# One pair of experts instead of two kept for the down products by columns at the end

## The chip, the core and the metric

The kernel runs on one core of a Trainium2 chip, in one launch. The metric is device time in microseconds (us). Its engines are TensorE (PE in the profile, with PEld for its weight loads), VectorE (DVE), ScalarE (ACT), GpSimd (POOL) and SyncE (SP), which issues the DMAs of the weights.

## The reference, cut to what matters

One encoder layer on 256 tokens of 1024 channels, all in float32: a mixer block, then a mixture of 32 experts, the residual and a last RMSNorm. The change touches the experts and the norm:

```python
for e in range(N_EXPERTS):                     # 32
    act = silu(t @ w1[e]) * (t @ w3[e])        # 1024 -> 512
    out = out + combine[:, e:e+1] * (act @ w2[e])   # 512 -> 1024
x = x + out
return rmsnorm(x, norm_final_g)
```

A token goes to two experts. The weights w1, w3 and w2 of one expert are 2 MiB each, 192 MiB in all.

## The kernel before

After the mixer and the routing the kernel works through 16 pairs of experts. At most 64 tokens are gathered for an expert (a general path, `general()`, L922, handles more behind a test at run time, and is jumped over here); the two experts of a pair share the 128 columns of every product.

A pair has these steps. `hidden` (L857) computes w1, then w3, 16 matmuls of 512 columns each in the program (the profile shows two passes for each float32 matmul, so 32). ACT applies silu, DVE multiplies (L884). `spread` (L834) transposes the pair's one-hot tokens. `turn` (L887) transposes the activations, and `down` (L901) multiplies them with w2, 16 matmuls of 512 columns. `two` (L896) splits each result in a rounded part (ACT, L897) and the rest (DVE, L898). `combine` (L915) scatters both parts to the 256 tokens with 8 matmuls into the four accumulators `accm`; the program puts it in the middle of the next pair's `hidden`. Every second pair also gathers the tokens of the next four experts (L790).

The weights come through a ring of 22 slots of 1 MiB, in the order of the list `stream` (L56 to L94), in DMAs from SP's queue (L124). A DMA waits until its slot is free and until an earlier DMA on its semaphore has landed; eight semaphores are used in turn. `fill` (L113) issues as many as there are free slots, and is called wherever a step frees some.

The last two pairs, 14 and 15, are treated apart. Their w2 is left out of `seq` (L75) and comes at the very end, in pieces of 256 and 128 columns, pair 14 and pair 15 in turns (L88 to L94). So the program computes w1 and w3 of pair 14, the first matrix of pair 15 with `turn_a` in the middle (L1010), jumps over the general path, adds the accumulators of pairs 0 to 13 to the residual (L1021), computes w3 of pair 15, and then runs the down products of both pairs by columns (`down_col` L1030, `combine_a` L1052, `combine_b` L1058). Behind a column group follow the residual (L1063), its squares (L1068) and, for the second half of the tokens, the product with the last norm's gain (L1071). That gain was spread over all partitions before, by `gains_bcast` (L998, L1001). At last come the sum of squares (L1096), the root, and five scaled pieces with their DMAs (L1106).

The program's order is the order written; no scheduler moves it. The lines that set it at the end are

```python
    a = hidden(NP - 2)
    gwa, gwb = [spread(gts[NP // 2 - 1], i) for i in range(2)]
    gains_bcast(0)
    gains_bcast(1)
    hidden(NP - 1, ("w1",), {("w1", 0): turn_a})
    general()
    ...
    a = hidden(NP - 1, ("w3",))
```

Of the kernel before, what the change touches and what calls it, by code (L numbers as in the profile page):

```python
# [9 lines left out]
FT = mybir.dt.float32  # L10
# [9 lines left out]
P = 128  # L20
# [20 lines left out]
def encoder_kernel(ctx, tc, x, norm_mix_g, w_in, conv_a_w, conv_b_w, conv_b_bias, ln_b_g, ln_b_b,  # L41
# [30 lines left out]
    w2_v = w2[0].rearrange("e (p k) d -> e p k d", k=KF)  # L72
    NP = E_ALL // 2
    W = {"w1": (w1_v, 4), "w3": (w3_v, 4), "w2": (w2_v, 2)}
    seq = [(pr, nm) for pr in range(NP) for nm in ("w1", "w3", "w2") if pr < NP - 2 or nm != "w2"]  # L75
    for q in range(4):
        for e in range(2):
            stream.append((("w1", e, q), w1_v[e][:, 2 * q:2 * q + 2, :], ("w1", q), e * 1024))
# [6 lines left out]
    for q in range(2):  # L85
        for e in (E_ALL - 2, E_ALL - 1):
            stream.append((("w3", e, 1 + q), w3_v[e][:, 4 + 2 * q:6 + 2 * q, :], ("w3", e), q * 1024))
    LAST2 = [(NP - 2, [(0, 256), (256, 256), (512, 256), (768, 256)]),  # L88
             (NP - 1, [(0, 256), (256, 256), (512, 256), (768, 128), (896, 128)])]
    COLS = LAST2[1][1]  # L90
    for i, c in [(0, 0), (1, 0), (0, 1), (1, 1), (0, 2), (0, 3), (1, 2), (1, 3), (1, 4)]:
        pr, (c0, n) = LAST2[i][0], LAST2[i][1][c]
        for e in (2 * pr, 2 * pr + 1):
            stream.append((("w2", e, c), w2_v[e][:, :, c0:c0 + n], ("w2", e, c0 // 512), c0 % 512 * KF))  # L94
    tiles, owner = {}, {}
    free = [(0, n) for n in range(RING)]
    order, shared = [1000], {}
# [2 lines left out]
    def slot(key, dt=FT, name="wt"):  # L100
        free.sort()
        owner[key] = free.pop(0)[1]
        return ring.tile([P, 2048], dt, name=name, tag=f"w{owner[key]}")

    def done(*keys, rank=None):
        for key in keys:
            order[0] += 1
            free.append((rank or order[0], owner.pop(key)))
# [805 lines left out]

    def combine(pr, gw, ys):  # L915
        for h in range(2):
            for nh in range(2):
                for n, y in enumerate(ys[nh]):
                    PE.matmul(accm[h][nh], gw[:, h], y, start=(pr == 0 and n == 0), stop=(pr == NP - 3 and n == 1))  # L919


    def general():  # L922
# [48 lines left out]
        done("gen", "tT")  # L971

    prev = None
    for pr in range(NP - 2):
        q, i = divmod(pr, 2)
        if i:
            gts[q + 1] = onehot(q + 1)
        keep[0] = int(pr == NP - 3)

        def mid():  # L980
            if prev:
                combine(*prev)
            else:
                fs[0] = factors(0, gt0)
        a = hidden(pr, meanwhile={("w1", 1): mid})
        gw = spread(gts[q], i)
        at = turn(a)
        if i:
            for n in range(4):
                gather(gts[q + 1], n)  # L990
            fs[q + 1] = factors(q + 1, gts[q + 1])
        prev = (pr, gw, down(pr, at))
    combine(*prev)
    done("x2h", "x2l")
    xl = slot("xl")
    gfb = xl[:, D:]

    def gains_bcast(nh):  # L998
        p = ps.tile([P, 512], FT, name="gfp", tag="mm")
        for k in range(4):  # L1000
            PE.matmul(p[:, k * P:(k + 1) * P], ident[0:KD, 4 * nh + k:4 * nh + k + 1].to_broadcast([KD, P]),  # L1001
                      gf8, start=True, stop=True)
        S.copy(gfb[:, nh * 512:(nh + 1) * 512], p)

    a = hidden(NP - 2)
    gwa, gwb = [spread(gts[NP // 2 - 1], i) for i in range(2)]
    gains_bcast(0)
    gains_bcast(1)

    def turn_a():  # L1010
        ats.append(turn(a, xl[:, 0:KF * P].rearrange("p (k t) -> p k t", k=KF)))

    ats = []

    hidden(NP - 1, ("w1",), {("w1", 0): turn_a})
    general()
    S.activation(warm, epst, AF.Sqrt)
    for h in range(2):
# [1 line left out]
            sl = slice(nh * 512, (nh + 1) * 512)  # L1020
            V.tensor_tensor(x1[:, h, sl], accm[h][nh], x1[:, h, sl], op=OP.add)  # L1021
    a = hidden(NP - 1, ("w3",))
    atl = turn(a, xl[:, KF * P:2 * KF * P].rearrange("p (k t) -> p k t", k=KF))
    s6 = cst.tile([P, 2, len(COLS)], FT, name="s6")
    xo = slot("xo").rearrange("p (h d) -> p h d", h=2)

    ysl = slot("ysl").rearrange("p (i n) -> p i n", n=256)
    ysr = slot("ysr", FR, "ysr").rearrange("p (i j n) -> p i j n", j=2, n=256)

    def down_col(i, c, at):  # L1030
        pr, cols = LAST2[i]
        n = cols[c][1]
        p = ps.tile([P, n], FT, name="yp", tag="mm")
        for k in range(KF):
            for e in range(2):
                PE.matmul(p[e * CAP:(e + 1) * CAP], at[:, k, e * CAP:(e + 1) * CAP],  # L1036
                          tiles["w2", 2 * pr + e, c][:, k], start=(k == 0), stop=(k == KF - 1))
        if c < 3:
            return two(p, ysr[:, (2 * c + i) % 4, 0], ysr[:, (2 * c + i) % 4, 1])
        ysb = ysl[:, 2 * (c % 4) + i, 0:n]  # L1040
        S.copy(ysb, p)
        return ysb

    def scatter(i, h, c, ysb, start, stop):
        g = (gwa, gwb)[i][:, h]
        parts = [(g, y) for y in ysb] if c < 3 else [(g.bitcast(FT), ysb)]
        for n, (g, y) in enumerate(parts):
            PE.matmul(pls[c, h], g, y, start=start and n == 0, stop=stop and n == len(parts) - 1)  # L1048

    pls = {}  # L1050

    def combine_a(c, ysb):  # L1052
        for h in range(2):
            pool, tag = (pacc, f"acc{h}{c % 2}") if c < 4 else (ps, "h")
            pls[c, h] = pool.tile([P, COLS[c][1]], FT, name="last", tag=tag)
            scatter(0, h, c, ysb, True, False)

    def combine_b(c, ysb):  # L1058
        c0, n = COLS[c]
        sl = slice(c0, c0 + n)  # L1060
        for h in range(2):
            scatter(1, h, c, ysb, False, True)
            V.tensor_tensor(x1[:, h, sl], pls[c, h], x1[:, h, sl], op=OP.add)  # L1063
            if h and c == len(COLS) - 1:
                V.scalar_tensor_tensor(ysl[:, 2, 0:n], x1[:, h, sl], 1.0, x1[:, h, sl], op0=OP.mult, op1=OP.mult,
                                       accum_out=s6[:, h, c:c + 1])
            else:
                S.activation(xo[:, 0, sl], x1[:, h, sl], AF.Square, accum_out=s6[:, h, c:c + 1])  # L1068

    def gains(c0, n, eng=V):  # L1070
        eng.tensor_tensor(xo[:, 1, c0:c0 + n], x1[:, 1, c0:c0 + n], gfb[:, c0:c0 + n], op=OP.mult)  # L1071

    yb, ya = {}, {}
    for c in range(2):
        ya[c] = down_col(0, c, ats[0])
        if c:
            combine_b(c - 1, yb[c - 1])
        yb[c] = down_col(1, c, atl)
        combine_a(c, ya[c])
    ya[2] = down_col(0, 2, ats[0])  # L1080
    combine_b(1, yb[1])
    gains(0, 256)
    ya[3] = down_col(0, 3, ats[0])
    combine_a(2, ya[2])
    combine_a(3, ya[3][:, 0:128])
    combine_a(4, ya[3][:, 128:256])
    gains(256, 256)
    yb[2] = down_col(1, 2, atl)
    yb[3] = down_col(1, 3, atl)
    combine_b(2, yb[2])  # L1090
    gains(512, 256, G)
    yb[4] = down_col(1, 4, atl)
    combine_b(3, yb[3])
    combine_b(4, yb[4])
    gains(768, 256, G)
    V.tensor_reduce(out=ss, in_=s6, axis=AX.X, op=OP.add)  # L1096
    S.activation(r2, ss, AF.Sqrt, bias=epst, scale=1.0 / D)  # L1097
    V.reciprocal(r2, r2)  # L1098
# [36 lines left out]
```

## Time and profile before

| what | value |
|---|---|
| median of 3 runs | 625.99 us (623.98 to 628.57) |
| the profiled execution's own time | 623.63 us |
| its span, first to last instruction | 621.9 us |
| mean granted TensorE clock | 0.952 of 2.4 GHz |
| PE busy | 555.0 us (89%) |
| DVE / ACT / POOL busy | 218.0 / 113.7 / 73.0 us |
| read from HBM | 217.30 MB, 351 GB/s over the span |

Times within the execution are counted from the start of the span. The page also cuts the span in 40 slices and gives the DMA share and GB/s of each; from about 165 us on DMA engines and PE are both busy nearly all the time, so the end of the kernel has to be read instruction by instruction, from the timeline.

### The profile page before, as it was taken

The page shows a single profiled execution, that of the slowest core. Times are in us where ns is not written, and L with a number is a line of the kernel's source. Part 1 is how long each engine was busy: PE and PEld are TensorE (multiplying, and loading weights), DVE is VectorE, ACT ScalarE, POOL GpSimd, SP SyncE. Part 2 cuts the span into 40 slices and gives each one's busy share as a digit, 9 for nine tenths or more (in the row PEclk, how much of TensorE's full clock was granted, in tenths as well). Part 3 has the DMA queues.
Part 4 walks back from the last instruction along what each step waited for, and adds up shares of the span by engine and source line. Part 5 has one row for each costly group of instructions (what it writes and reads, how often), then busy time and mean ns, then how long its engine had stood idle before and what let it go on. Part 6 is the DMA issues. An engine that isn't in the chain of part 4 may idle for free. (4 is left out here: it accounts for less than half of the span.)

```text
span 621.9 us, 7346 instructions
## 1 busy us (share of the span) xinstructions
PE 555.0 (89%) x2966; PEld 300.5 (48%) x2966; DVE 218.0 (35%) x392; ACT 113.7 (18%) x230; POOL 73.0 (12%) x53
## 2 busy tenths in 40 slices
PE   6939496799899999999999999999999999999795
PEld 5939396457644533443453335345333533534253
DVE  5799999864711202120120203012010301210232
ACT  3542041445411010000101000010100100001123
POOL 1776372610000000000000000000000000000000
PEclk8977697899799999999999999999999999999998
DMA  8990091853499999999999999999999999999992
GB/s 289 346 391 4 21 393 61 338 185 127 190 416 420 421 422 419 422 421 422 422 421 421 420 422 420 420 422 421 420 422 420 421 420 422 421 423 421 374 332 83
DMA packets 48776, 218.85 MB, mean 352 GB/s; under 512 B 6061, under 2 KB 19645, under 8 KB 25956
## 3 DMA queue, kind: packets, MB, share of 16 engines
q1 hardware_dynamic: 48554, 218.28, 87.5%
q8 instruction: 24, 0.39, 0.3%
q10 hardware_dynamic: 186, 0.08, 0.0%
q14 instruction: 12, 0.10, 0.0%
HBM read 217.30 MB, written 1.05 MB: 351 GB/s over the span
## 5 line engine op out<-in xcount | busy, mean ns | idle before, releaser
L869 PE MATMUL ph<-wt 128*64 128x512 f32 x1024 | 229.7, 598 | 3.3 <-PEq L924 3.3
L869 PEld LDWEIGHTS ph<-wt 128*64 128x64 f32 x1024 | 77.2, 138 | 142.7 <-issue 133.8
L908 PE MATMUL yp<-wt,at 128*64 128x512 f32 x448 | 99.2, 595 | 7.6 <-issue 5.8
L310 DVE SCALAR_TENSOR_TENSOR vb<-wt,prm,vb 128x256 f32<-128x256 f32 x120 | 90.3, 809 | 0.9
L884 DVE SCALAR_TENSOR_TENSOR sl<-ph,fs,sl 128x512 f32<-128x512 f32 x16 | 12.0, 751 | 217.6 <-PE ph L869 217.6
L908 PEld LDWEIGHTS yp<-wt,at 128*64 128x64 f32 x448 | 34.0, 137 | 62.5 <-issue 59.5
L293 PE MATMUL pj<-xhi,whi 128*128 128x256 f32 x128 | 36.3, 313 | 21.4 <-DVE wt L342 21.4
L1071 POOL TENSOR_TENSOR wt<-x,wt 128x256 f32<-128x256 f32 x2 | 1.6, 776 | 457.9 <-DVE x L1063 457.9
L898 DVE TENSOR_TENSOR yl<-yp,yh 128x512 fp32r<-128x512 f32 x28 | 19.4, 692 | 100.5 <-ACT yh L897 100.5
L267 POOL TENSOR_TENSOR wlo<-wt,whi 128x2048 fp32r<-128x2048 f32 x10 | 47.4, 4758 | 19.6 <-ACT whi L261 11.9
L293 PEld LDWEIGHTS pj<-xhi,whi 128*128 128x128 f32 x128 | 28.3, 221 | 21.8 <-DVE wt L342 21.8
L294 PE MATMUL pj<-xlo,whi 128*128 128x256 f32 x128 | 35.8, 310 | 0.0
L897 ACT CAST yh<-yp 128x512 fp32r<-128x512 f32 x28 | 16.4, 585 | 104.5 <-PE yp L908 104.5
L882 ACT ACTIVATE sl<-ph,fs 128x512 f32<-128x512 f32 x16 | 11.0, 687 | 101.1 <-PE ph L869 101.0
L839 ACT CAST gw<-gwp 128x256 fp32r<-128x256 f32 x16 | 5.9, 372 | 125.4 <-PE gwp L837 125.4
L294 PEld LDWEIGHTS pj<-xlo,whi 128*128 128x128 f32 x128 | 28.3, 221 | 0.0
L790 PE MATMUL gp<-gt,x2h 128*128 128x256 f32 x112 | 24.3, 298 | 0.0
L919 PE MATMUL acc<-yh,gw 128*128 128x512 f32 x56 | 23.6, 421 | 0.0
L791 DVE TENSOR_TENSOR wt<-gp,g 128x512 f32<-128x512 f32 x28 | 19.4, 692 | 8.5 <-PE gp L790 8.5
L919 PE MATMUL acc<-yl,gw 128*128 128x512 f32 x56 | 22.1, 394 | 0.2 <-DVE yl L898 0.2
L790 PE MATMUL gp<-gt,x2l 128*128 128x256 f32 x112 | 22.2, 279 | 0.0
L261 ACT CAST whi<-wt 128x2048 fp32r<-128x2048 f32 x10 | 18.9, 1900 | 14.3 <-PE pj L298 12.1
(232 smaller groups left out, 507.6 us busy)
## 6 DMA issues: line engine op xcount, KB each, us to landing
wt<-in_w_dram SPq DMA_DIRECT2D x178, 1024.0 KB, 19.8
wt<-in_w_dram SPq DMA_DIRECT2D x26, 512.0 KB, 9.7
wt<-in_w_in_dram SPq DMA_DIRECT2D x10, 1024.0 KB, 9.0
wt<-in_w_out_dram SPq DMA_DIRECT2D x4, 1024.0 KB, 10.6
x<-in_x_dram SPq DMA_DIRECT2D x2, 512.0 KB, 6.2
wt<-in_w_dram SPq DMA_DIRECT2D x4, 256.0 KB, 8.2
out_dram<-x SPq DMA_DIRECT2D x3, 256.0 KB, 2.1
out_dram<-x SPq DMA_DIRECT2D x2, 128.0 KB
```

What stands on the lines that cost most here:

```text
L261: S.copy(h_, w)
L267: eng.tensor_tensor(l_, w, hi[key].bitcast(FT), op=OP.subtract)
L293: PE.matmul(p, w, xhi[:, k], start=(k == 0), stop=False)
L294: PE.matmul(p, w, xlo[:, k], start=False, stop=False)
L310: V.scalar_tensor_tensor(a, ub[:, b, j:j + T], w(j), a, op0=OP.mult, op1=OP.add)
L790: PE.matmul(p[:, k], xs[:, h, 2 * q + k], g[:, h], start=(n == 0), stop=(n == 3))
L791: V.tensor_tensor(xg[:, 2 * q:2 * q + 2], p, g2[:, 2 * q:2 * q + 2, None].to_broadcast([P, 2, 4 * CAP]), op=OP.mult)
L869: PE.matmul(p[e * CAP:(e + 1) * CAP], xg[:, k, c0 + e * CAP:c0 + (e + 1) * CAP], w, start=(k == 0), stop=(k == KD - 1))
L897: S.copy(yh, p)
L898: V.tensor_tensor(yl, p, yh.bitcast(FT), op=OP.subtract)
L908: PE.matmul(pn[nh][e * CAP:(e + 1) * CAP], at[:, k, e * CAP:(e + 1) * CAP], w[:, k % 2, nh * 512:(nh + 1) * 512], start=(k == 0), stop=(k ...
L919: PE.matmul(accm[h][nh], gw[:, h], y, start=(pr == 0 and n == 0), stop=(pr == NP - 3 and n == 1))
```

## The change

Only pair 15 is now treated apart. Pair 14 becomes a pair like the others: its w2 stands in `seq` behind its w3, in pieces of 1 MiB, and its `down` and `combine` are the usual ones, into the accumulators. The last pair's w2 comes in columns 0 to 511, 512 to 767 and 768 to 1023, the last of these in two halves of the 512 inner rows. `combine` of pair 14, `spread` of pair 15 and the spreading of the gain all stand behind the last matmul of w1 of pair 15 (`mid_last`), ahead of the test. In the tail each column group runs down product, split, scatter, residual, squares and gain before the next begins.

```diff
-    seq = [(pr, nm) for pr in range(NP) for nm in ("w1", "w3", "w2") if pr < NP - 2 or nm != "w2"]
+    seq = [(pr, nm) for pr in range(NP) for nm in ("w1", "w3", "w2") if pr < NP - 1 or nm != "w2"]
...
-    LAST2 = [(NP - 2, [(0, 256), (256, 256), (512, 256), (768, 256)]),
-             (NP - 1, [(0, 256), (256, 256), (512, 256), (768, 128), (896, 128)])]
-    for i, c in [(0, 0), (1, 0), (0, 1), (1, 1), (0, 2), (0, 3), (1, 2), (1, 3), (1, 4)]:
+    COLS = [(0, 512), (512, 256), (768, 256)]
+    for c, (c0, n) in enumerate(COLS):
+        for kh in range(2 if c == 2 else 1):
+            nk = KF // 2 if c == 2 else KF
+            for e in (E_ALL - 2, E_ALL - 1):
+                stream.append((("w2", e, c, kh), w2_v[e][:, nk * kh:nk * (kh + 1), c0:c0 + n],
+                               ("w2", e, c0 // 512), (c0 % 512 * KF + nk * kh * n)))
...
-    for pr in range(NP - 2):
+    for pr in range(NP - 1):
...
-        keep[0] = int(pr == NP - 3)
...
+        if pr == NP - 3:
+            done("x2h", "x2l")
+            xl = slot("xl")
+            xo = slot("xo").rearrange("p (h d) -> p h d", h=2)
         prev = (pr, gw, down(pr, at))
-    combine(*prev)
-    done("x2h", "x2l")
-    xl = slot("xl")
...
-    a = hidden(NP - 2)
-    gwa, gwb = [spread(gts[NP // 2 - 1], i) for i in range(2)]
-    gains_bcast(0)
-    gains_bcast(1)
...
-    hidden(NP - 1, ("w1",), {("w1", 0): turn_a})
+    def mid_last():
+        combine(*prev)
+        gwl.append(spread(gts[NP // 2 - 1], 1))
+        gains_bcast(0)
+        gains_bcast(1)
+
+    hidden(NP - 1, ("w1",), {("w1", 1): mid_last})
     general()
...
+    def down_col(c):
+        n = COLS[c][1]
+        p = ps.tile([P, n], FT, name="yp", tag="mm")
+        nk = KF // 2 if c == 2 else KF
         for k in range(KF):
             for e in range(2):
...
+        yh, yl = [wk.tile([P, 512], FR, name=nm, bufs=2)[:, 0:n] for nm in ("yh", "yl")]
+        return two(p, yh, yl)
+
+    def combine_col(c, ys):
+        c0, n = COLS[c]
+        sl = slice(c0, c0 + n)
+        for h in range(2):
+            p = pacc.tile([P, n], FT, name="last", tag=f"acc{h}{c % 2}")
+            for i, y in enumerate(ys):
+                PE.matmul(p, gwl[0][:, h], y, start=(i == 0), stop=(i == 1))
+            V.tensor_tensor(x1[:, h, sl], p, x1[:, h, sl], op=OP.add)
...
+    for c in range(NC_):
+        combine_col(c, down_col(c))
+        gains(c, G if c == NC_ - 1 else V)
```

Three places show how instructions move. In them `wt` is a slot of the ring, `ph` the hidden product, `yp` the down product, `gfp` the spread gain, `tp` the transposed activations, `last` the scatter in the tail, and `cint` the number that the test reads.

SP's queue, the end of the stream before (128x2048 is 1 MiB in one DMA):

```order
L124 DMA wt<-in_w_dram 128x1024 x8
L124 DMA wt<-in_w_dram 128x2048 x178
L124 DMA wt<-in_w_dram 128x1024 x4
L124 DMA wt<-in_w_dram 128x4x256 x14
L124 DMA wt<-in_w_dram 128x4x128 x4
L923 TENSOR_LOAD cint
```

and now:

```order
L125 DMA wt<-in_w_dram 128x2048 x182
L125 DMA wt<-in_w_dram 128x1024 x4
L125 DMA wt<-in_w_dram 128x4x512 x2
L125 DMA wt<-in_w_dram 128x4x256 x2
L125 DMA wt<-in_w_dram 128x2x256 x4
L924 TENSOR_LOAD cint
```

Four pieces of 1 MiB more stand ahead of the last pair's w1 and w3, and the pieces by columns are 8 instead of 18.

PE from the hidden products of pair 14 to the test, before:

```order
L869 MATMUL ph<-wt 64x512 x32
L837 MATMUL gwp<-ident,gt 128x128 x4
L1001 MATMUL gfp<-gf_105,ident 128x128 x8
L869 MATMUL ph<-wt 64x512 x8
L891 MATMUL tp<-ident,sl 128x128 x4
L869 MATMUL ph<-wt 64x512 x8
L923 TENSOR_LOAD cint
L924 COMPARE_AND_BRANCH
```

Now, from w3 of pair 14 to the first scatter of pair 14:

```order
L870 MATMUL ph<-wt 64x512 x16
L838 MATMUL gwp<-ident,gt 128x128 x2
L892 MATMUL tp<-ident,sl 128x128 x4
L909 MATMUL yp<-wt,at 64x512 x16
L870 MATMUL ph<-wt 64x512 x16
L920 MATMUL acc_1388<-yh,gw 128x512
```

and from its last scatter to the test:

```order
L920 MATMUL acc_1391<-yh,gw 128x512
L920 MATMUL acc_1391<-yl,gw 128x512
L838 MATMUL gwp<-ident,gt 128x128 x2
L1003 MATMUL gfp<-gf_105,ident 128x128 x8
L924 TENSOR_LOAD cint
L925 COMPARE_AND_BRANCH
```

The down product of pair 14 stands ahead of w1 of pair 15, and its scatter, one spread and the gain stand between that w1 and the test.

PE in the tail, before (the first rows from w3 of pair 15 on):

```order
L869 MATMUL ph<-wt 64x512 x16
L891 MATMUL tp<-ident,sl 128x128 x4
L1036 MATMUL yp<-wt 64x256 x16
L1048 MATMUL last<-ysr,gw 128x256 x4
L1036 MATMUL yp<-wt 64x256 x8
L1048 MATMUL last<-ysr,gw 128x256 x4
```

and now:

```order
L870 MATMUL ph<-wt 64x512 x16
L892 MATMUL tp<-ident,sl 128x128 x4
L1034 MATMUL yp<-wt 64x512 x8
L1045 MATMUL last<-yh,gw 128x512
L1045 MATMUL last<-yl,gw 128x512
L1045 MATMUL last<-yh,gw 128x512
L1045 MATMUL last<-yl,gw 128x512
L1034 MATMUL yp<-wt 64x256 x8
```

Before, PE always had the next group's down product between a group's down product and its scatter; now the scatter follows its own group at once.

## Rows read from the trace of the kernel before

**Rows 1.** The page: busy time by engine; DMA share in 40 slices (tenths).

```profile
PE 555.0 (89%) x2966; PEld 300.5 (48%) x2966; DVE 218.0 (35%) x392; ACT 113.7 (18%) x230; POOL 73.0 (12%) x53
...
DMA  8990091853499999999999999999999999999992
```

**Rows 2.** Busy time by stretch: us, engines, granted clock, DMA share, GB/s.

```profile
530.00:560.00 30.00, 28.92 (x155) 13.04 (x155) 5.59 (x8) 1.70 (x4) 0.00 (x0) 1.00 1.01 420
...
585.00:590.00 5.00, 5.00 (x26) 1.95 (x24) 1.74 (x3) 0.00 (x0) 0.00 (x0) 1.00 1.09 348
...
600.00:605.00 5.00, 5.00 (x40) 3.12 (x40) 1.42 (x5) 1.76 (x6) 0.00 (x0) 1.00 1.12 334
605.00:610.00 5.00, 5.00 (x43) 3.60 (x44) 1.63 (x5) 1.39 (x5) 0.00 (x0) 1.00 0.43 122
```

**Rows 3.** Timeline of SP, 569 to 571 us: start, duration, what.

```profile
569.47 0.33 SPq L124 DMA_DIRECT2D wt<-in_w_dram  x1
```

**Rows 4.** DMAs issued from 569 to 571 us: KB, us to landing.

```profile
wt<-in_w_dram SPq DMA_DIRECT2D x1, 512.0 KB, 15.1
```

**Rows 5.** Timeline of PE, pair 12: start, duration, what, passes, idle before.

```profile
502.15 0.50 PE L919 MATMUL acc<-yh,gw 128*128 128x512 f32 x1
...
504.18 7.09 PE L869 MATMUL ph<-wt 128*64 128x512 f32 x32
511.20 0.44 PE L837 MATMUL gwp<-ident,gt 128*128 128x128 f32 x2
...
513.80 7.09 PE L908 MATMUL yp<-wt,at 128*64 128x512 f32 x32 [0.83 <-issue]
```

**Rows 6.** Timeline of PE, pair 13's scatter to the tail.

```profile
551.91 0.50 PE L919 MATMUL acc<-yh,gw 128*128 128x512 f32 x1
...
569.57 2.05 PE L1001 MATMUL gfp<-gf,ident 8*128 8x128 f32 x16 [0.24 <-ACT gw L839]
571.54 5.35 PE L869 MATMUL ph<-wt 128*64 128x512 f32 x16
...
577.51 3.65 PE L869 MATMUL ph<-wt 128*64 128x512 f32 x16
584.43 7.09 PE L869 MATMUL ph<-wt 128*64 128x512 f32 x32 [3.27 <-PEq L924]
...
593.11 3.67 PE L1036 MATMUL yp<-wt 128*64 128x256 f32 x32
...
597.38 1.95 PE L1036 MATMUL yp<-wt 128*64 128x256 f32 x16
```

**Rows 7.** Groups by line and shape, 500 to 622 us: busy us, mean ns.

```profile
L898 DVE TENSOR_TENSOR yl<-yp,yh 128x512 fp32r<-128x512 f32 x4 | 2.8, 692 | 14.4 <-ACT yh L897 14.4
...
L898 DVE TENSOR_TENSOR ysr<-yp,ysr 128x256 fp32r<-128x256 f32 x6 | 2.5, 425 | 12.9 <-ACT ysr L897 11.3 <-DMA wt<-in_w_dram 1.6
...
L897 ACT CAST yh<-yp 128x512 fp32r<-128x512 f32 x4 | 2.3, 585 | 14.9 <-PE yp L908 14.9
...
L1063 DVE TENSOR_TENSOR x<-last,x 128x256 f32<-128x256 f32 x6 | 2.2, 416 | 0.5 <-PE last L1048 0.5
...
L897 ACT CAST ysr<-yp 128x256 fp32r<-128x256 f32 x6 | 2.2, 372 | 20.6 <-PE yp L1036 20.6
```

**Rows 8.** Timeline of all engines, the sum of squares at the end.

```profile
615.02 0.16 DVE L1096 TENSOR_REDUCE ss<-s 128x2 f32<-128x10 f32 x1
```

**Rows 9.** The test's line: durations in ns (min/median/max), start.

```profile
L924 PEldq COMPARE_BRANCH  x1: 5992/5992/5992, 578.1 to 578.1; - x1
...
L924 ACTq COMPARE_BRANCH  x1: 45/45/45, 581.8 to 581.8; - x1
```

**Rows 10.** Busy time by stretch, around the test.

```profile
571.50:577.00 5.50, 5.50 (x18) 1.64 (x18) 0.00 (x0) 0.58 (x1) 0.00 (x0) 0.69 1.01 419
...
581.20:584.40 3.20, 0.00 (x0) 0.00 (x1) 0.14 (x1) 2.17 (x3) 0.00 (x0) 1.00 1.06 369
```

**Rows 11.** What SP's queue waited for, 480 to 622 us: us, times, longest.

```profile
SPq L124 <- PE ph L869: 3.3, 3, 2.6
```

More of the change, by code (lines that the diff above doesn't have):

```diff
@@ L87, in encoder_kernel @@
             stream.append((("w3", e, 1 + q), w3_v[e][:, 4 + 2 * q:6 + 2 * q, :], ("w3", e), q * 1024))
-    LAST2 = [(NP - 2, [(0, 256), (256, 256), (512, 256), (768, 256)]),
-             (NP - 1, [(0, 256), (256, 256), (512, 256), (768, 128), (896, 128)])]
-    COLS = LAST2[1][1]
-    for i, c in [(0, 0), (1, 0), (0, 1), (1, 1), (0, 2), (0, 3), (1, 2), (1, 3), (1, 4)]:
-        pr, (c0, n) = LAST2[i][0], LAST2[i][1][c]
-        for e in (2 * pr, 2 * pr + 1):
-            stream.append((("w2", e, c), w2_v[e][:, :, c0:c0 + n], ("w2", e, c0 // 512), c0 % 512 * KF))
+    COLS = [(0, 512), (512, 256), (768, 256)]
[5 more added lines that the diff above has]
+                               ("w2", e, c0 // 512), (c0 % 512 * KF + nk * kh * n)))
     tiles, owner = {}, {}
@@ L918, in combine @@
                 for n, y in enumerate(ys[nh]):
-                    PE.matmul(accm[h][nh], gw[:, h], y, start=(pr == 0 and n == 0), stop=(pr == NP - 3 and n == 1))
+                    PE.matmul(accm[h][nh], gw[:, h], y, start=(pr == 0 and n == 0), stop=(pr == NP - 2 and n == 1))
     def general():
@@ L973, in encoder_kernel @@
     prev = None
-    for pr in range(NP - 2):
+    for pr in range(NP - 1):
         q, i = divmod(pr, 2)
-        if i:
+        more_ = i and pr < NP - 1
+        if more_:
             gts[q + 1] = onehot(q + 1)
-        keep[0] = int(pr == NP - 3)
         def mid():
@@ L987, in encoder_kernel @@
         at = turn(a)
-        if i:
+        if more_:
             for n in range(4):
@@ L1003, in gains_bcast @@
         S.copy(gfb[:, nh * 512:(nh + 1) * 512], p)
-    a = hidden(NP - 2)
-    gwa, gwb = [spread(gts[NP // 2 - 1], i) for i in range(2)]
-    gains_bcast(0)
-    gains_bcast(1)
-    def turn_a():
-        ats.append(turn(a, xl[:, 0:KF * P].rearrange("p (k t) -> p k t", k=KF)))
-    ats = []
-    hidden(NP - 1, ("w1",), {("w1", 0): turn_a})
+    gwl = []
+    def mid_last():
[4 more added lines that the diff above has]
+    hidden(NP - 1, ("w1",), {("w1", 1): mid_last})
     general()
@@ L1022, in encoder_kernel @@
     a = hidden(NP - 1, ("w3",))
[L1023 to L1032, printed above, removed]
+    atl = turn(a, xl[:, 0:KF * P].rearrange("p (k t) -> p k t", k=KF))
+    NC_ = len(COLS)
+    s6 = cst.tile([P, 2, NC_], FT, name="s6")
+    def down_col(c):
+        n = COLS[c][1]
         p = ps.tile([P, n], FT, name="yp", tag="mm")
+        nk = KF // 2 if c == 2 else KF
         for k in range(KF):
             for e in range(2):
[L1036 to L1058, printed above, removed]
+                PE.matmul(p[e * CAP:(e + 1) * CAP], atl[:, k, e * CAP:(e + 1) * CAP],
+                          tiles["w2", E_ALL - 2 + e, c, k // nk][:, k % nk], start=(k == 0), stop=(k == KF - 1))
+        yh, yl = [wk.tile([P, 512], FR, name=nm, bufs=2)[:, 0:n] for nm in ("yh", "yl")]
+        return two(p, yh, yl)
+    def combine_col(c, ys):
         c0, n = COLS[c]
@@ L1061, in combine_b @@
         for h in range(2):
[L1062 to L1065, printed above, removed]
+            p = pacc.tile([P, n], FT, name="last", tag=f"acc{h}{c % 2}")
+            for i, y in enumerate(ys):
+                PE.matmul(p, gwl[0][:, h], y, start=(i == 0), stop=(i == 1))
+            V.tensor_tensor(x1[:, h, sl], p, x1[:, h, sl], op=OP.add)
+            if h and c == NC_ - 1:
+                V.scalar_tensor_tensor(xl[:, 512:512 + n], x1[:, h, sl], 1.0, x1[:, h, sl], op0=OP.mult, op1=OP.mult,
                                        accum_out=s6[:, h, c:c + 1])
@@ L1068, in combine_b, with gains @@
                 S.activation(xo[:, 0, sl], x1[:, h, sl], AF.Square, accum_out=s6[:, h, c:c + 1])
-    def gains(c0, n, eng=V):
+    def gains(c, eng=V):
+        c0, n = COLS[c]
         eng.tensor_tensor(xo[:, 1, c0:c0 + n], x1[:, 1, c0:c0 + n], gfb[:, c0:c0 + n], op=OP.mult)
[L1073 to L1095, printed above, removed]
+    for c in range(NC_):
+        combine_col(c, down_col(c))
+        gains(c, G if c == NC_ - 1 else V)
     V.tensor_reduce(out=ss, in_=s6, axis=AX.X, op=OP.add)
```

## The prediction

> **What bounds the kernel now.** I read the page first, then the stretches, then PE's timeline, because two resources are nearly full at once. The page gives PE 89% of the span, and from the twelfth slice on a DMA share of nine tenths or more [rows 1]. Up to 580 us the stretches say it finer: from 530 to 560 us PE is busy 28.92 of 30 us, and the DMAs move 420 GB/s with a share of 1.01 [rows 2]. So the stream of weights runs at its full rate, and a step of PE can start no sooner than its weights have landed. At the end this changes. When the pieces by columns come, the rate drops to 348 and 334 GB/s, and the stream is done before 610 us [rows 2], but PE works without a gap from 593.11 us on [rows 6]: there PE, not the stream, sets the end. SP waits for a slot that PE holds only 3.3 us in the last 140 us [rows 11]; the ring does not hold the stream back.
>
> Two places decide the change. The first is the landing of the last weights ahead of w3 of pair 15. The second is the time from the start of that w3 to the sum of squares.
>
> **The gate.** Before, the last piece of w3 of pair 15 is issued at 569.47 us and lands 15.1 us later, at 584.6 us [rows 3, 4]. Ahead of it in the stream stand all weights but the w2 of pairs 14 and 15. The change puts the 4 MiB of pair 14's w2 ahead of pair 15's w1, so at the place of that piece there now stands the last piece of **w1** of pair 15. The bytes up to there are the same, and the rate is the stream's own, so w1's second half cannot start before 584.6 us.
>
> Is PE there by then? It leaves pair 13's down product at 551.91 us [rows 6]. Then come w1 of pair 14 (7.09), pair 13's scatter (502.15 to 504.18, so 2.03), w3 (7.09), spread, product and turn (511.20 to 513.80, so 2.60) and the down product (7.09) [rows 5]. That is 25.90 us, to 577.8 us. PE could end w1 of pair 15 at 584.9 us; the weights make it wait. From 584.6 us the second half takes 7.09 / 2 = 3.5 us, to 588.1 us.
>
> **From the gate to w3.** Behind w1 stand, on PE and in this order, pair 14's scatter (2.03), one spread (at most 0.44, the row of two transposes [rows 5]) and the gain (2.05 [rows 6]), which makes 592.6 us, and then the test. Before, PE's last matmul ahead of the test ended at 577.51 + 3.65 = 581.16 us, and w3 began at 584.43 us [rows 6]: 3.3 us in which PE did nothing. The same jump now stands behind the gain. I take 3.3 us again, so w3 begins at 595.9 us, when its own weights are there: its 4 MiB follow the gate at about 420 GB/s, 10 us, and land by 594.6 us. Against 584.43 us that is **11.5 us later**.
>
> What else moved past something costs nothing here. ACT copies the gain ahead of the silu of w1, but that silu is used only at the end of w3. DVE's four additions of the accumulators still wait for the jump and have all of w3 (7.09 us) as cover. SP reads the test's number behind its last weight DMA, and nothing waits for SP before the output. The two slots that `xl` and `xo` take early leave the stream 22 - 3 = 19, as many as while x2h, x2l and xg were held. If that cover failed, SP's waits for PE would grow beyond the 3.3 us.
>
> **The tail.** Before, 30.6 us pass from the start of w3 to the sum of squares, 584.43 to 615.02 us [rows 6, 8]. Now pair 14's down products and scatters are gone from it. From w3's start to the first down product it stays 593.11 - 584.43 = 8.7 us [rows 6]. The first group, 512 columns, is half a down product, 3.5 us. Its scatter needs ACT's rounding (0.585) and then DVE's rest (0.692) [rows 7], and PE has nothing else to do: 1.4 us with the steps between, and then three of four scatter passes at 2.03 / 8 = 0.25, so 0.75. Group two: 1.95 us [rows 6], an exposed split of 0.372 + 0.425 [rows 7], 0.9 with the steps, and 0.4 for the passes at half the width. Group three the same, up to its last scatter. Then come on DVE the residual of the second half (0.416 [rows 7]), the squares, which I price like the residual of that shape, and some 0.1 us for the accumulator. Sum: 8.7 + 3.5 + 1.4 + 0.75 + 3.25 + 3.25 + 0.95 = 21.8; I take 22.2 us, as ACT's squares of the first group, 512 wide, stand ahead of group two's rounding. That is **8.4 us less**.
>
> The column weights are no gate. Their 4 MiB follow at 334 to 420 GB/s, 10 to 12.6 us, so the last lands by 607 us; the last group starts near 613 us. The new pieces by columns bring the stream's end forward, but nothing waits for it.
>
> **The clock.** At 571.5 us, right behind the gain's matmuls (8 rows of the array, 2.05 us), the granted clock fell to 1.2 GHz, and half of w1 took 5.35 us in place of 3.65 us [rows 6]; that stretch shows 0.69 on average [rows 10]. Behind the idle 3.2 us of the test the clock stayed at 2.4 GHz [rows 10]. Now spread, gain and idle test follow each other, 5.8 us with hardly any work, so I expect the fall, on w3: 5.35 - 3.65 = **1.7 us**. Before, the same fall lay on w1 of pair 15, and is contained in the start of w3 at 584.43 us.
>
> **Sum:** 11.5 - 8.4 + 1.7 = **4.8 us more**. The profiled execution took 623.63 us; it would take 628.4 us. Of the four executions shown (623.63, 623.98, 625.99, 628.57) it is the fastest. The median of the four is 625.0 us, 1.0 us under the median of the three runs, and on it I put the forecast: 629.8 us.
>
> **What I cannot see, with both ends.** The jump: ACT's took 45 ns, PE's record 5.99 us, from the sequencer's arrival on [rows 9]; so 0.3 to 6.0 us in place of 3.3, that is -3.0 to +2.7. I take 3.3, the same engine's at the same jump. The fall: none (-1.7) to all of w3 at half speed (7.1 - 1.7 = +5.4); I take what one fall cost here. The gate: none, if the stream were early, lets PE reach w3 3.2 us sooner (584.9 + 2.03 + 0.44 + 2.05 + 3.3 = 592.7); later it can hardly be, as the bytes ahead of it are the same. The exposed splits: 0 to 3.2 us; 3.2 is taken, since PE's order leaves nothing to put there.
>
> **Rivals.**
> *The jump costs its whole record* (0.18). PE's sequencer reached the branch at 578.1 us, 3 us ahead of the array's end, and the record runs 6 us. If those 6 us are the price of the jump and half of it was hidden under w1, then now less is hidden, as the last matmuls ahead of it are short and wait for each other. Against it: the jump could as well wait for the array. Up to 2.7 us more: 632.5 us, slower by 1.2%. It decides from 1.5 us on.
>
> *The clock does not fall* (0.17): 628.1 us. For it speaks the idle stretch that was followed by a full clock; against it the stretch behind the gain.
>
> *Not slower: the gate or the jump vanishes* (0.13). If w1 of pair 15 is there when PE wants it, 3.2 us go; if the jump is as short as ACT's, 3.0 us go. With the fall still there the time is 626.6 to 626.8 us, without it 625.0 us, no change. The Trainium skill ("Runtime: NRT & Kernel Launch", section on instruction fetch mechanics) says that a taken branch stalls only if its target lies outside the pages already fetched; that would let the jump's price change with where the code lies. The 45 ns of ACT against PE's 3.3 us agree that both kinds occur.
>
> *The stream sets the end* (0.07). If column groups really wait for their weights, which the gapless PE from 593.11 us on speaks against, the end follows the stream. Of the last 8 MiB half now come at 420 in place of some 335 GB/s: 4.19 MB take 10.0 in place of 12.5 us, and of the other half, two MiB come in rows of twice the length, 6.3 us at 335 and 5.0 us at 420, so another 1.3 us at most. That is 3.8 us earlier, 621.2 us. The Trainium skill ("DMA: Bandwidth & Descriptors", section Rules for kernel authors) asks for at least 1 MiB in one DMA, and by that rule alone the change would be a gain. The rates in this trace agree with it; PE's timeline says that this is not where the time is.
>
> The forecast itself has 0.45.
>
> **Range and chances.** The forecast and the cases beside it reach from 625.0 us (no change) to 632.5 us. On the upper side I add 1.5 us, as the four executions scatter more above their median than below, and on the lower 1 us, which gives 624.0 to 634.0 us. That leaves out the stream's case and a clock that stays low for all of w3. About 1%, 6.3 us, is what a measurement of this kernel can tell from no change. The forecast is 0.8% above 625.0 us, so most of its chance lies within 1%; a quarter of it and nearly all of the first rival lie beyond: slower 0.29. Faster takes the part of the stream's case in which it and the vanished jump go together, 0.05, and 0.66 stays for the same.
>
> **What the profile after would show.** w1 of pair 15 in two halves with a gap, the second from about 584.6 us; w3 starting near 595.9 us with some 3 us of idle PE ahead, and its first passes at twice the usual distance; PE idle about 0.7 us before each scatter's first pass and again before its second; the weight stream ended by 607 us; the sum of squares near 619.7 us. The forecast is wrong if w3 starts before 593 us, or if the tail from there takes more than 25 us, or if PE waits for the column pieces.

## The result, and the profile after

| | median of 20 runs | lowest to highest |
|---|---|---|
| before | 626.53 us | 623.41 to 631.15 |
| the change | 629.74 us | 626.66 to 634.66 |

The ratio is 1.0053, with a 95% interval of 1.0027 to 1.0078: the change costs 3.2 us (1.7 to 4.9).

Two executions of the change were profiled. The first took 634.66 us, the longest of its 20; the second (run `e11_change_again` below) took 630.82 us, near the median, and I read the steps there. The page of the second, busy time and DMA share, answers to [rows 1]:

```profile
PE 556.6 (89%) x2882; PEld 297.1 (47%) x2882; DVE 218.9 (35%) x387; ACT 112.2 (18%) x218; POOL 72.5 (12%) x52
...
DMA  8990190854399999999999999999999999999961
```

PE has 84 instructions fewer and is no less busy, and the stream is as full as before. What changed is the end. PE's timeline there, second profile (start, us, what, passes, idle before and who ended it), answers to [rows 6]:

```profile
582.35 3.65 PE L870 MATMUL ph<-wt 128*64 128x512 f32 x16 [0.87 <-DMA wt<-in_w_dram]
...
587.32 3.65 PE L870 MATMUL ph<-wt 128*64 128x512 f32 x14 [1.32 <-DMA wt<-in_w_dram]
590.90 0.50 PE L920 MATMUL acc<-yh,gw 128*128 128x512 f32 x1
...
593.16 2.05 PE L1003 MATMUL gfp<-gf,ident 8*128 8x128 f32 x16
596.51 8.50 PE L870 MATMUL ph<-wt 128*64 128x512 f32 x32 [1.31 <-ACTq L925]
...
607.48 3.65 PE L1034 MATMUL yp<-wt 128*64 128x512 f32 x16 [0.79 <-DVE wt L894]
...
611.81 0.51 PE L1045 MATMUL last<-yh,gw 128*128 128x512 f32 x1 [0.69 <-ACT yh L898]
...
612.54 0.50 PE L1045 MATMUL last<-yl,gw 128*128 128x512 f32 x1 [0.22 <-DVE yl L899]
...
613.43 1.95 PE L1034 MATMUL yp<-wt 128*64 128x256 f32 x16
...
615.85 0.38 PE L1045 MATMUL last<-yh,gw 128*128 128x256 f32 x1 [0.47 <-ACT yh L898]
```

Both halves of w1 (582.35, 587.32) now wait for a DMA: the landing gate. w3 starts at 596.51, where before it started at 584.43 us, and waits last not for PE's own sequencer, as in [rows 6], but for ACT. DVE's sum of squares closes the tail (it answers to [rows 8]), 6.5 us later than before:

```profile
621.49 0.16 DVE L1060 TENSOR_REDUCE ss<-s 128x2 f32<-128x6 f32 x1
```

Not all 6.5 us belong to the change. Pair 0 already starts later, in both profiles of the change (the other shows 168.27). PE's timeline at pair 0, before first, then the second profile of the change:

```profile
166.36 7.09 PE L869 MATMUL ph<-wt 128*64 128x512 f32 x32
```

```profile
168.23 7.61 PE L870 MATMUL ph<-wt 128*64 128x512 f32 x32
```

These 1.9 us lie ahead of the experts, in code that the change does not touch; in the kernels below that are built on the change and leave the mixer alone, pair 0 starts between 166.50 and 168.80 us. Most of them come from the clock. From 163 to 169 us the granted clock is 1.00 before and 0.50 in both profiles of the change, and the passes that gather the first tokens take 0.41 in place of 0.28 us (before first):

```profile
165.98 0.28 PE L763 MATMUL gp<-gt,x2h 128*128 128x256 f32 x1
```

```profile
165.88 0.41 PE L764 MATMUL gp<-gt,x2h 128*128 128x256 f32 x1
```

Why the clock rose later there is open. Pair 0's w1 then takes 7.61 in place of 7.09 us, and when pair 14 begins, the first place where PE's order differs, the change is 2.75 us behind: PE left pair 13's down product at 551.91 us before [rows 6] and at 554.66 us now.

```profile
554.66 7.04 PE L870 MATMUL ph<-wt 128*64 128x512 f32 x32
```

I take the 2.75 us off. From there the change costs 6.5 - 2.8 = **3.7 us** in this pair of profiles.

The stretches of the second profile (us, busy time of PE, PEld, DVE, ACT, POOL, granted clock, DMA share, GB/s) answer to [rows 2, 10]:

```profile
595.00:600.00 5.00, 3.69 (x12) 1.15 (x13) 2.48 (x4) 2.66 (x4) 0.00 (x0) 0.66 1.05 384
...
605.00:610.00 5.00, 3.29 (x18) 1.48 (x18) 1.44 (x2) 0.00 (x0) 0.00 (x0) 1.00 0.28 98
```

The clock falls at the start of w3. The stream ends before 610 us, as before, and nothing on PE waits for a DMA behind that.

### The profile page after: what moved, and what is told of

The parts are those of the page before. It is cut to its first block, busy times and chain, and to the rows that moved or that the text cites. A ratio compares the mean times of both kernels' runs of the same rounds, so it can differ in the third digit from the quotient of the medians.

```text
span 631.8 us, 7128 instructions
## 1 busy us (share of the span) xinstructions
PE 559.3 (89%) x2882; PEld 298.0 (47%) x2882; DVE 219.1 (35%) x387; ACT 112.3 (18%) x218; POOL 72.7 (12%) x52
## 5 line engine op out<-in xcount | busy, mean ns | idle before, releaser
L870 PE MATMUL ph<-wt 128*64 128x512 f32 x1024 | 233.1, 602 | 4.0 <-DMA wt<-in_w_dram 2.7
L870 PEld LDWEIGHTS ph<-wt 128*64 128x64 f32 x1024 | 78.5, 139 | 145.8 <-issue 134.0
L909 PE MATMUL yp<-wt,at 128*64 128x512 f32 x480 | 106.7, 595 | 8.4 <-issue 6.6
L909 PEld LDWEIGHTS yp<-wt,at 128*64 128x64 f32 x480 | 36.7, 137 | 67.3 <-issue 64.1
L899 DVE TENSOR_TENSOR yl<-yp,yh 128x512 fp32r<-128x512 f32 (+1 forms) x33 | 22.3, 676 | 116.1 <-ACT yh L898 116.1
L898 ACT CAST yh<-yp 128x512 fp32r<-128x512 f32 (+1 forms) x33 | 18.9, 572 | 130.2 <-PE yp L909 113.1
L294 PEld LDWEIGHTS pj<-xhi,whi 128*128 128x128 f32 x128 | 28.2, 220 | 22.1 <-DVE wt L343 22.1
L920 PE MATMUL acc<-yh,gw 128*128 128x512 f32 x60 | 25.2, 420 | 0.0
L920 PE MATMUL acc<-yl,gw 128*128 128x512 f32 x60 | 23.6, 393 | 0.0
L791 PE MATMUL gp<-gt,x2l 128*128 128x256 f32 x112 | 22.2, 279 | 0.0
```

What stands on the lines that cost most here:

```text
L294: PE.matmul(p, w, xhi[:, k], start=(k == 0), stop=False)
L791: PE.matmul(p[:, k], xs[:, h, 2 * q + k], g[:, h], start=(n == 0), stop=(n == 3))
L870: PE.matmul(p[e * CAP:(e + 1) * CAP], xg[:, k, c0 + e * CAP:c0 + (e + 1) * CAP], w, start=(k == 0), stop=(k == KD - 1))
L898: S.copy(yh, p)
L899: V.tensor_tensor(yl, p, yh.bitcast(FT), op=OP.subtract)
```

## The experiments

Ratios are to the kernel before, run on the same chip in the same batch (its medians: 626.28, 626.18 and 625.58 us), with their 95% intervals. The change itself was not run in these batches but for e11; "under the change" sets a ratio against its 1.0053 above. Gaps behind w1 are counted from the start of its last pass.

**e1: gain and spread earlier.** The short matmuls go ahead of pair 14's down product; only the scatter stays ahead of the test.

```diff
 def mid_last():
     combine(*prev)
-    gwl.append(spread(gts[NP // 2 - 1], 1)); gains_bcast(0); gains_bcast(1)
...
+        if pr == NP - 2:
+            gwl.append(spread(gts[NP // 2 - 1], 1)); gains_bcast(0); gains_bcast(1)
         prev = (pr, gw, down(pr, at))
```

> The changed kernel, with the last pair's spread and the two matmul groups of the gain moved ahead of pair 14's down product; behind w1 of pair 15 only pair 14's scatter is left ahead of the test. Theory 1 (the stretch between w1 and w3 of pair 15 holds both the chain of gain, ACT copies and silu, and the lack of work that lets the clock fall): w3 starts about 3 us after w1's last matmul in place of 5.5, the granted clock stays at 2.4 GHz through w3 and the first column group, so 2.5 us and up to 4.7 us go; time 4 to 7 us under the changed kernel, ratio to the kernel before 0.994 to 0.999. Rival (the clock falls because of the idle test alone): 2.5 us go, ratio 1.001. Rival (the gate alone costs what was lost): nothing goes, ratio 1.005.

Measured: 626.40 us, 1.0006 [0.9989, 1.0024], 2.9 us under the change. PE's timeline and stretches of this kernel:

```profile
575.18 8.78 PE L909 MATMUL yp<-wt,at 128*64 128x512 f32 x32
...
593.16 7.09 PE L870 MATMUL ph<-wt 128*64 128x512 f32 x32 [0.30 <-ACT warm L1019]
```

```profile
575.00:580.00 5.00, 5.00 (x19) 1.55 (x19) 0.00 (x0) 0.59 (x1) 0.00 (x0) 0.66 1.01 419
...
595.00:600.00 5.00, 5.00 (x26) 1.81 (x22) 0.48 (x1) 0.00 (x0) 0.00 (x0) 1.00 1.05 384
```

w3 keeps the full clock and starts 2.9 us behind w1's last pass (6.1 in both profiles of the change). The fall went with the gain: pair 14's down product now takes 8.78 us. That is mostly hidden in the time in which PE waited for w1's weights in the change; here w1 shows no such wait and ends at the same place (the scatter starts at 590.76, in the change at 590.90 us). So the fall here follows the gain's matmuls and not the test, and what the change put between gate and w3, the fall on w3 included, is worth about 3 us.

**e2: the next group's down product ahead of the scatter.**

```diff
+    ys = down_col(0)
     for c in range(NC_):
-        combine_col(c, down_col(c))
+        nys = down_col(c + 1) if c < NC_ - 1 else None
+        combine_col(c, ys)
         ...
+        ys = nys
```

> The changed kernel, with each column group's down product issued ahead of the scatter of the group before it. Theory 1 (the exposed splits of a group cost PE 0.9 us for the first and 0.5 us for the others, 1.9 us in the trace): two of three are covered, 1.4 us go, ratio to the kernel before 1.003. Rival (the tail is bound by the chain of ACT and DVE from group to group): less than 0.5 us go. Rival (idle PE between the groups lets the clock fall on the first group): up to 3 us go.

Measured: 626.75 us, 1.0009 [0.9990, 1.0028], about 2.7 us under the change. PE's timeline:

```profile
596.63 8.73 PE L870 MATMUL ph<-wt 128*64 128x512 f32 x32 [1.31 <-ACTq L925]
...
607.83 5.38 PE L1034 MATMUL yp<-wt 128*64 128x512 f32 x32 [0.79 <-DVE wt L894]
```

Two groups run as one, and from w3's start to the sum of squares (619.44) it takes 22.8 us in place of 25.0. The exposed splits were real. The gain is more than the 1.4 us expected; where the rest comes from I did not settle.

**e3, e4: the same kernels, with the code moved.** More warm-up transposes on PE at the start of the kernel shift all later PE instructions, in before by 80 and in the change by 176.

```diff
-for _ in range(14):
+for _ in range(14 + 40):        # e3, before;  e4, the change: 14 + 88
```

> The kernel before, with 40 more transposes of the identity in the warm-up at its start, whose 80 instructions put the test's branch where the changed kernel has it in PE's code. Theory 1 (PE's branch took 6 us before and 0.5 us in the changed kernel because of where its code lies in the blocks that are fetched): the branch takes under 1 us, w3 of pair 15 starts within 1 us of ACT's silu of w1 in place of 3.3 us after the last matmul, 2 to 3 us go, ratio 0.995 to 0.997. Rival (the branch is slow because matmuls of w1 still run when it is reached): it stays at 5 to 6 us and the time is the same, or some tenths longer by the warm-up.

> The changed kernel, with 88 more transposes of the identity in the warm-up, whose 176 instructions put the branch where the kernel before has it in a block of PE's code. Theory 1 (the place in the code decides): the branch record grows from 0.46 to some 6 us and w3 of pair 15 starts about 3 us later after w1 than in the changed kernel. Rival (what runs at the time decides): the branch stays under 1 us.

Measured: e3 626.81 us, 1.0005 [0.9987, 1.0024]; e4 640.66 us, 1.0231 [1.0198, 1.0264], from two executions only. PE's branch at the test (duration in ns, start), answering to [rows 9], and w3 of pair 15: first e3, then e4, then the second profile of the change. (The row of e4's w3 holds the first 18 passes; all 32 take 9.56 us.)

```profile
L924 PEldq COMPARE_BRANCH  x1: 445/445/445, 583.3 to 583.3; - x1
```

```profile
587.23 7.09 PE L869 MATMUL ph<-wt 128*64 128x512 f32 x32 [0.86 <-ACTq L924]
```

```profile
L925 PEldq COMPARE_BRANCH  x1: 6267/6267/6267, 599.4 to 599.4; - x1
```

```profile
606.01 6.55 PE L870 MATMUL ph<-wt 128*64 128x512 f32 x18 [5.68 <-PEq L925]
```

```profile
L925 PEldq COMPARE_BRANCH  x1: 458/458/458, 594.3 to 594.3; - x1
```

The record of the same jump is 0.45 or 6 us long by where its code lies, and moving the code exchanged the two. In e3 w3 follows w1's last pass by 1.45 in place of 3.9 us. The time did not follow in e3: its pair 0 starts at 170.13 in place of 166.36 us. Of these 3.8 us, 1.75 are the longer warm-up (the first projection starts at 13.39 in place of 11.64 us); for the rest, the clock stays at 0.50 from 163 to 169 us here as well. In e4 pair 0 starts 5.8 us late as well (174.02); the other 5 us of its 10.9 lie at the jump and in a clock fall that lasts from 600.8 to 611.0 us.

**e5: before, with the code moved at no cost.** The same 40 transposes stand in the mixer instead, where PE is idle for 9.3 us.

```diff
+        if b:
+            dumb = pacc.tile([P, 512], FT, name="dumb", tag="acc11")
+            for _ in range(40):
+                PE.transpose(dumb[:, 0:P], ident, ident)
         S.copy(ca[:, b + 1], proj("c", b + 1))
```

> The kernel before with the same 40 transposes, now at a place of the mixer where PE waits 9.3 us for DVE (ahead of the last projection of the group c), so that they take no time of their own. Theory 1 (the branch at its old place in the code costs the kernel before some 2.4 us, which the warm-up of the run before hid): branch under 0.5 us, w3 of pair 15 starts about 2.4 us earlier relative to the end of w1, ratio to the kernel before 0.995 to 0.997. Rival (w3 of pair 15 is then held by its own weights, which land at 584.6 us): less than 1 us goes, ratio 0.998 to 1.000.

Measured: 624.09 us, 0.9962 [0.9945, 0.9980]. Branch and timeline:

```profile
L928 PEldq COMPARE_BRANCH  x1: 1305/1305/1305, 578.7 to 578.7; - x1
```

```profile
571.84 2.05 PE L1005 MATMUL gfp<-gf,ident 8*128 8x128 f32 x16 [0.24 <-ACT gw L843]
573.81 3.65 PE L873 MATMUL ph<-wt 128*64 128x512 f32 x16
...
582.59 7.42 PE L873 MATMUL ph<-wt 128*64 128x512 f32 x32 [0.86 <-ACTq L928]
...
596.51 2.38 PE L1040 MATMUL yp<-wt 128*64 128x256 f32 x16
...
599.50 2.34 PE L1040 MATMUL yp<-wt 128*64 128x256 f32 x16
```

That is 2.4 us by the ratio, without any work moved, but it is not the jump alone. The gain stands in one piece as before, and in this profile the clock did not fall behind it (1.00 from 560 to 616 us): the first half of w1 took 3.65 in place of 5.35 us. So from pair 13's scatter to w3 it takes 4.1 us less, 2.4 by the jump and 1.7 by the clock. The column groups now follow each other every 2.99 us, where before it was 2.54 (597.38 [rows 6] to 599.92). Their 1 MiB at the 348 GB/s of [rows 2] is 3.0 us: with an earlier start and a full clock they run at the pace of the stream, and 2.9 of the 4.1 us are lost again up to the sum of squares (616.09 us). Why the clock held here is open.

**e6: dense matmuls behind the gain, to keep the clock up.**

```diff
         gains_bcast(1)
+        keepc = ps.tile([P, 512], FT, name="keepc", tag="mm")
+        for n in range(8):
+            PE.matmul(keepc, prev[1][:, 0], prev[2][0][0], start=(n == 0), stop=(n == 7))
```

> The changed kernel, with 8 dense matmuls of 512 columns (repeated products that nobody reads) behind the gain, where PE has nothing to do until ACT's silu has ended. Theory 1 (the clock falls for the lack of dense work between w1 and w3): w3 and the first column group run at 2.4 GHz; of the 4.7 us that the falls took in the trace of the changed kernel 3 or more go, less some 1 us by which the 1.9 us of matmuls outlast the wait for ACT; ratio to the kernel before 1.000 to 1.003. Rival (the fall has nothing to do with this stretch): ratio 1.006 to 1.007.

Measured: 630.81 us, 1.0069 [1.0042, 1.0096], the rival's number. PE's timeline:

```profile
593.72 2.80 PE L1016 MATMUL keepc<-yh,gw 128*128 128x512 f32 x8
596.82 7.82 PE L870 MATMUL ph<-wt 128*64 128x512 f32 x32 [0.30 <-PEq L925]
```

The clock fell all the same (594.9 to 598.3 us), now on the added matmuls, which took 0.35 us each (2.80 / 8), where the scatter's of that shape take 0.25, and on w3. And w3 starts 7.9 us behind w1's last pass in place of 6.1. Work added behind the gain did not prevent the fall.

**e7, e9: the gain split between dense halves.** Its two halves stand between the halves of w1 and of w3 of pair 14; the spread of pair 15 stands behind pair 14's turn. e7 has e2's tail too, e9 has the tail of the change.

```diff
+        between = {("w1", 1): mid}
+        if pr == NP - 2:
+            between["w1", 0] = lambda: gains_bcast(0)
+            between["w3", 0] = lambda: gains_bcast(1)
-        a = hidden(pr, meanwhile={("w1", 1): mid})
+        a = hidden(pr, meanwhile=between)
```

> The changed kernel, with the gain's two matmul groups put between the halves of w1 and of w3 of pair 14, the spread of pair 15 behind the turn of pair 14, and each column group's down product ahead of the scatter of the group before. Theory 1 (gain, clock and exposed splits are separate costs): no fall of the clock between 540 us and the tail, w3 of pair 15 starts 3 us after w1, two splits covered; 6 to 8 us under the changed kernel, ratio to the kernel before 0.993 to 0.996. Rival (earlier work only makes PE wait longer for the last weights): not below 0.998.

> The changed kernel with the gain's two groups between the halves of w1 and of w3 of pair 14 and the spread of pair 15 behind the turn of pair 14; the tail is the changed kernel's. It differs from the first run (gain ahead of pair 14's down product, 1.0006) by the place of the gain alone. Theory 1 (8-row matmuls in one stretch with the turn let the clock fall on pair 14's down product, 1.7 us, of which the wait for w1's last weights hid a part): no fall there, 0.5 to 1.7 us less than the first run, ratio to the kernel before 0.997 to 1.000. Rival (the wait for the weights hid all of it): 1.0006 as in the first run.

Measured: e7 623.07 us, 0.9951 [0.9929, 0.9972]; e9 624.23 us, 0.9984 [0.9963, 1.0005]. PE's timeline of e7, then a stretch of e9, to be set beside e1's:

```profile
584.87 3.65 PE L870 MATMUL ph<-wt 128*64 128x512 f32 x14 [0.23 <-DMA wt<-in_w_dram]
...
590.88 7.09 PE L870 MATMUL ph<-wt 128*64 128x512 f32 x32 [0.30 <-ACT warm L1021]
```

```profile
575.00:580.00 5.00, 5.00 (x25) 1.92 (x24) 0.00 (x0) 0.00 (x0) 0.00 (x0) 1.00 1.02 423
```

In e7, and in the same way in e9, no fall of the clock in the experts: in e7 it is full from 163.0 us to 613.6. Half of the gain between two dense halves (8 passes, 1.15 us) is not followed by a fall; the whole in one place was in eight of the nine profiles that have it so, and was not in e5. In e7 the sum of squares comes at 612.87: against before w3 starts 6.4 us later, and the tail of 22.0 us is 8.6 shorter, so the balance is -2.2. e9 and e1 differ by the place of the gain, and their intervals overlap: that the fall on the down product costs anything in e1 is not shown.

**e8: the test ahead of w1 as well.** e7 with `general()` ahead of pair 15's w1, and e5's transposes, meant to keep the jump short there.

```diff
+general()
 hidden(NP - 1, ("w1",), {("w1", 1): mid_last})
-general()
```

> The run before it (gain between the halves, overlapped tail), with the test ahead of w1 of pair 15, where PE waits for weights, and the 40 transposes of the identity in the mixer's idle place, so that the branch stays where it is cheap. Theory 1 (behind w1 only pair 14's scatter is then left): w3 starts about 2.1 us after w1, 0.9 us less, ratio 0.991 to 0.995. Rival (w3's own weights, 10 us behind w1's, hold it): the same as the run before it.

Measured: 622.01 us, **0.9927** [0.9900, 0.9955], the lowest of all, 1.2% under the change; its interval overlaps e7's. Part of it needs no new order: e5, the kernel before with the same transposes, took 624.09 us in the same batch. PE's timeline:

```profile
582.23 4.51 PE L874 MATMUL ph<-wt 128*64 128x512 f32 x18 [0.83 <-ACTq L929]
...
586.95 3.65 PE L874 MATMUL ph<-wt 128*64 128x512 f32 x14 [0.22 <-DMA wt<-in_w_dram]
592.58 7.09 PE L874 MATMUL ph<-wt 128*64 128x512 f32 x32
```

Between w1 and w3 only the scatter is left, 2.0 us, and w3 follows it without a wait. The branch (2.8 us here) lies ahead of the gate.

**e10: the gate itself, by swapping w1 of pair 15 with w2 of pair 14**, in the stream and on PE, on top of e8.

```diff
+seq = seq[:-3] + [seq[-2], seq[-3], seq[-1]]
```

> The best version so far (gain between the halves, test early, overlapped tail, 0.9927), with the stream's order of the change undone for one step: w1 of pair 15 ahead of w2 of pair 14, in the stream and on PE, and pair 14's scatter between the halves of w3. Theory 1 (the landing of w1's last weights at 584.6 us is the gate, with half of w1, the scatter and all of w3 behind it): now pair 14's second half of the down product stands behind that landing in place of w1's, its split is covered by the first half of w3, and w3 ends 1.5 to 2 us earlier, held by its own last weights (594.6 us); ratio 0.990 to 0.992. Rival (the gate is worth nothing once PE has work to fill): 0.992 to 0.994.

Measured: 624.62 us, 0.9980 [0.9964, 0.9996]; slower than e8, a miss for both theories (e8 was run in another batch). PE's timeline:

```profile
586.93 3.22 PE L914 MATMUL yp<-wt 128*64 128x512 f32 x13 [1.40 <-DMA wt<-in_w_dram]
...
591.90 3.65 PE L875 MATMUL ph<-wt 128*64 128x512 f32 x14 [1.31 <-DMA wt<-in_w_dram]
...
597.51 3.65 PE L875 MATMUL ph<-wt 128*64 128x512 f32 x16
...
603.55 7.08 PE L1045 MATMUL yp<-wt 128*64 128x512 f32 x32 [0.78 <-DVE wt L899]
```

w1 is no longer held, but the down product and then w3 are, by 1.40 and 1.31 us, and pair 14's scatter now stands behind that second gate. The clock fell from 604.0 to 607.4 us, far behind the split gain, and the first column groups took 7.08 in place of 5.84 us in e8; what brought this fall is open. The bytes ahead of w3 are the same in any order; an exchange only chooses which step stands behind the gate.

**e11: the change once more**, unaltered, for a profile nearer the median.

> The changed kernel, profiled a second time, since its first profile was one of its slowest executions (634.7 us against a median of 629.7). What is asked is how long the clock falls in w3 of pair 15 and in the first column group: 2.9 and 1.8 us were lost there in the first profile. Theory 1 (the place of the fall differs from run to run, and the first profile shows much of it): 1.3 to 3 us in all. Rival (4.7 us each time): the same again.

Measured: 630.82 us (one run); its rows are those at the top. The clock's loss differs from the first profile, where w3 took 10.01 us (7.09 at full clock) and the first column group 5.35 (3.65 at full clock):

```profile
596.91 10.01 PE L870 MATMUL ph<-wt 128*64 128x512 f32 x32 [1.31 <-ACTq L925]
...
609.38 5.35 PE L1034 MATMUL yp<-wt 128*64 128x512 f32 x16 [0.78 <-DVE wt L894]
```

## Why the prediction was right, and where not

629.8 us was forecast and 629.74 measured, but that is nearer than the working deserves. The base, 625.0 us from four executions, was 1.5 us under the 626.53 of 20, and the step up, 4.8 us, was 1.6 more than the 3.2 between the medians. The two errors cancel. Step by step, in the second profile against before:

**The gate: right.** Forecast 584.6 us; w1's second half starts at 587.32, which is 584.6 with the 2.75 us by which PE was late already at pair 14. The distance holds elsewhere too: from the end of pair 13's down product to this row it is 32.6 to 32.7 us in both profiles of the change and in e2, e4, e6, e7 and e9, where the forecast has 584.6 - 551.9 = 32.7 (in e8, with the test ahead of w1, it is 33.8). From there to the end of the gain it takes 7.9 us (587.32 to 595.21), forecast 8.0. e7 adds a detail: with the gain done earlier, PE waits only 0.23 us for the second half, so PE and stream arrive there almost together.

**The jump: this step failed.** "I take 3.3 us again" supposed that the price goes with the jump. It goes with the code's place: the change moved the code, PE's branch took 0.46 us in place of 5.99, and e3, e4 and e5 show both prices in both kernels. The rival "the jump vanishes" had the mechanism, with the Trainium skill's page "Runtime: NRT & Kernel Launch", section on instruction fetch mechanics, beside it: a taken branch to a page not yet fetched waits for a fetch. The runs agree with it; that the 1.3 and 2.8 us of e5 and e8 are the rest of a fetch already under way is only argued. The opposite rival, that the whole record is paid, is false for this layout and nearly true in e4, where PE stood idle for 5.68 of the record's 6.27 us.

**In its place a wait for ACT.** I had put at nothing that ACT copies the gain ahead of the silu. ACT's timeline, second profile:

```profile
594.35 0.59 ACT L1005 COPY wt<-gfp 128x512 f32<-128x512 f32 x1 [0.71 <-PE gfp L1003]
595.24 0.59 ACT L1005 COPY wt<-gfp 128x512 f32<-128x512 f32 x1 [0.31 <-PE gfp L1003]
595.72 0.69 ACT L883 ACTIVATE sl<-ph,fs 128x512 f32<-128x512 f32 x1
```

The silu ends at 596.41 and PE goes on at 596.51: the profile puts PE's wait at the test down to ACT's queue, whose last work there is the silu. So 3.3 us became 1.3, and w3 started 12.1 - 2.8 = 9.3 us later, where 11.5 was forecast.

**The tail: right in kind, 1.4 us short.** Forecast 22.2 us with the clock full. Measured 596.51 to 621.49, 25.0, less 1.4 for the clock in w3 (8.50 against 7.09), is 23.6. Of the missing 1.4 us, 0.9 lie between w3 and the first down product: 607.48 - 596.51 - 1.41 = 9.56 in place of 8.7. There PE now waits 0.79 us for DVE's copy of the turn. Before, pair 14's down product stood in that place and covered it, and I carried over the covered figure. The other 0.5 lie in the groups, and not in the exposed splits: PE waits 0.69 + 0.22 and then 0.47 us for them, less than the 1.4 and 0.9 that were priced, but from the first scatter pass to the next down product it takes 1.6 us, 1.4 without the wait in it, where 0.75 was priced. The prediction's own sign of being wrong, a tail of more than 25 us, is just missed here; in the first profile, with the longer fall of the clock, the tail took 28.2 us.

**The clock: right for w3, too exact on the size.** Forecast 1.7 us on w3; measured 1.4 in the second profile and 2.9 + 1.7 = 4.6 in the first, on w3 and the first group. That the fall on w3 goes with the gain's matmuls is borne out by e1 (the fall moves with them) and e7 and e9 (split, there is none). It isn't the whole rule: in e5 the gain in one piece was not followed by a fall, and the falls on the first column group, in the first profile and in e10, have no gain right ahead of them.

**The sum.** 9.3 us later at w3, and the tail 30.6 before and 25.0 now, 5.6 less: 9.3 - 5.6 = 3.7, where 4.8 was forecast. Of a jump 2.0 us shorter than forecast, a tail that was 1.4 longer used up the most; the clock gave 0.3 back, and the steps ahead of the test 0.2. Between the medians it is 3.2 us. The two profiles differ by more, 6.5 us, for the 2.75 us that lie ahead of pair 14; before's profiled execution, at a full clock there, was near the lowest of its 20.

**The stream: right.** It still ends before 610 us and no column group waits for it, so that rival is dead for the change. e5 shows how near it was for the kernel before: with w3 1.8 us earlier (582.59 us) the column groups did run at the stream's pace. And e1, e7 and e9, where w3 of the change starts earlier, wait 0.5 to 0.7 us for a DMA in the first column group.

## What to carry to other kernels

Bytes put ahead in a full stream delay the landing of all that stands behind them; here w3 came 9.3 us later, and it pays only if more than that falls away behind it (e8, where the delay was cut and the tail shortened, is 0.7% faster than before, with some of it from the moved code). Look at what stands between a step that waits for the stream and the next one: scatter, gain, jump and silu took 5.5 us there (590.97 to 596.51), and most of it could go to places where engines waited anyway. Before taking a jump's price from a trace, look at its branch record, and count on another price as soon as the code moves; and where a step takes another's neighbour away, ask which wait that neighbour covered.

## What the runs showed of the hardware

One taken branch of PE took 0.45 to 6.3 us in kernels that differ only in where its code lies (before with e3 and e5, the change with e4); ACT's, DVE's and POOL's at the same test took 45 to 76 ns. Transposes added in an idle place, which move the code, made the kernel before 0.4% faster, in a profile in which the clock did not fall either.

TensorE's clock fell from 2.4 to 1.2 GHz behind 2.05 us of matmuls that use 8 of 128 rows in eight of nine profiles in which they stood in one piece (not in e5), and 8 dense matmuls right behind them did not prevent it (e6). Split in two, each half between dense matmuls, they were not followed by a fall there (e7 to e10); e10's clock fell 36 us later. Two executions of the same kernel lost 1.4 and 4.6 us to falls behind the test. Ahead of pair 0 the clock rose at about 163 us in some profiles and at about 169 us in others, which alone put the experts some 2 us later.
